# Key and value projections of a cross-attention stage as joint pairs: the last k-group by seven products, one core of a Trainium2 chip

## The chip, the cores and the metric

The kernel runs on one core of one Trainium2 chip. The core has a matrix engine (PE; its weight loads are listed apart as PEld), a vector engine (DVE), a scalar engine (ACT), a general-purpose engine (POOL) and a sync engine (SP) that issues most DMAs. Each engine works through its own instructions in a fixed order and waits on semaphores for the others. The metric is the device time of one execution in microseconds; less is better. About 0.2% (5.4 us here) is what a measurement of this kernel can tell from no change.

## The reference, cut to what matters

Two transformer blocks run one after the other on 256 tokens of width 2048, all in float32. The change lies in the memory cross-attention of the second block:

```python
def memory_cross_attention(h, mem_n, w_cq, w_ckv, w_co):
    q = (h @ w_cq).reshape(B, T, CROSS_HEADS, CROSS_HD)          # 4 heads of 512
    kv = (mem_n @ w_ckv).reshape(B, M, 2, CROSS_HEADS, CROSS_HD)
    k, v = kv[:, :, 0], kv[:, :, 1]
    s = jnp.einsum('bthd,bmhd->bhtm', q, k).astype(jnp.float32) * (CROSS_HD ** -0.5)
    pr = jax.nn.softmax(s, axis=-1).astype(v.dtype)
    o = jnp.einsum('bhtm,bmhd->bthd', pr, v).reshape(B, T, D_MODEL)
    return o @ w_co
```

`mem_n` is 256 memory rows of width 2048, normalised; `w_ckv` is 2048 x 4096. Columns 512h to 512h+511 give the keys of head h, columns 2048+512h onward its values.

## The kernel before

**Tiles.** A weight matrix is read in units of 512 rows x 512 columns (1 MB, one DMA into a `raw` tile; four of those exist). A unit is four k-tiles of 128 rows. A chunk is 512 output columns: its four units are the k-groups g = 0 to 3. Float32 precision is kept by splitting every operand in a high and a low part of type fp32r: ACT casts the high part (L235, `wh`), DVE subtracts to get the low one (L236, `wl`), half a unit (128 x 1024) at a time, at most five halves ahead (`WBUF`). A product of one k-tile then takes three matmuls of 512 columns (L280 to L282) for each of the two token tiles t, so a unit costs 24 matmuls.

**Pairs and seven products.** Two chunks that read the same activations can be computed as a pair (`pair8`). For k-groups 0 to 2 each chunk's units run as usual into four accumulators `c11`, `c21` (left chunk, token tiles 0 and 1) and `c12`, `c22` (right chunk). For the last k-group the two units and the activations are seen as a 2 x 2 times 2 x 2 block product, which Strassen's and Winograd's scheme does with seven block products in place of eight. Seven times six matmuls stand in place of 48. The price is paid elsewhere: DVE forms sums of weight blocks (`form`, four operations of 128 x 1024), seven halves are split in place of four, the activations' block sums are made once (`sums_job`, `four_sums`), and the results are put together by one copy on ACT (L376) and eight adds on DVE: L378 (first rows of the left chunk, tile `a`), L381, L383, L384 (`b`), L387, L389 (second rows of the left chunk, tile `c`), L391, L392 (second rows of the right chunk, tile `u`). The last of the seven products goes into `c21`, and L389 is the add that waits for it. `w_cq`, `w_in` and the first chunk of both feed-forwards already run in this way; `w_ckv` does not.

**The cross stage.** `cross` computes the four query chunks as two pairs. Then `gemm` (before) walks through eight chunks of `w_ckv` in the order key 0, value 0, key 1, value 1 and so on. When a key chunk is done, `on_k` scales it by the memory rows' normalisation on ACT (L505, `scaled`) and starts a `group_job`, which some k-tiles later (`wait`) flips it on PE (eight transposes, L490) and splits it (L472 on ACT, L473 on DVE). When the value chunk is done, `on_v` scales and splits the values (L1174, L1175) and starts `cross_job`: 24 matmuls of 256 columns for the scores S, softmax, four transposes (L1204), 24 matmuls for the output. `residual` then multiplies by `w_co`.

**What sets the order.** PE's order is the order in which the Python code emits instructions (`manual_schedule`); the other engines' order is set by the tile scheduler at build time and is fixed as well. Work beside the main stream is written as generators (jobs): `tick` after each k-tile lets each job count down its `yield n` and emit its next step. `spawn` runs a job's first step at once. `need(job)` runs a job to its end on the spot, whatever its wait. `cross_job` begins with `qT, kT = self.need(qT), self.need(kT)`.

Of the kernel before, what the change touches and what calls it, by code (L numbers as in the profile page):

```python
# [10 lines left out]
F32 = mybir.dt.float32  # L11
F32R = mybir.dt.float32r
# [71 lines left out]
class _Net:  # L84
# [87 lines left out]
    def plan(self):  # L172

        p, U = [], self.units
        self.seven = set()

        def add(chunks, late=False):
            p.extend(chunks[c][g] for c, g in self.order(chunks, late))

        def pair(a, b, seven):  # L180
            for g in range(len(a)):
                if g in seven:
                    self.seven.add(len(p))
                p.extend((b[g], a[g]))

        def ffn(gate, up, off, down, seven):
            for c, n, ks in self.ffn_steps():
                if n is not None:
                    add([U(down, n, ks)])
                else:  # L190
                    pair(U(gate, c), U(up, c + off), seven if c else (3,))
            add([U(down, n, PARTS[-1]) for n in range(4)])

        add([U("w_qkv", n) for n in (4, 0, 1, 2, 3)])
        add([U("w_o", n) for n in range(4)], True)
        ffn("w_gate", "w_up1", 0, "w_dn1", SEVEN1)
        for n in (0, 2, 6, 4):
            pair(U("w_in", n), U("w_in", n + 1), (3,))
        for ns in BRANCH:
            for n in ns:  # L200
                pair(U("w_in", 8 + n), U("w_in", 12 + n), (3,))
            add([U("w_br", n, (2 * j, 2 * j + 1)) for n in ns for j in range(2)])
        add([U("w_out", n) for n in range(4)], True)
        for n in (0, 2):
            pair(U("w_cq", n), U("w_cq", n + 1), (3,))
        add([U("w_ckv", 4 * j + h) for h in range(4) for j in range(2)])
        add([U("w_co", n) for n in range(4)], True)
        ffn("w_up2", "w_up2", 11, "w_dn2", SEVEN2)
        return p
# [113 lines left out]
            yield 2  # L323
        return out

    def four_sums(self, p, q):
        nc = self.nc
        s = self.s4([128, 8, 128])
        nc.vector.tensor_add(s[:, 0:2], q[:, 0:2], q[:, 2:4])
        nc.vector.tensor_sub(s[:, 2:4], s[:, 0:2], p[:, 0:2])  # L330
        nc.vector.tensor_sub(s[:, 4:6], p[:, 0:2], q[:, 0:2])
        nc.vector.tensor_sub(s[:, 6:8], p[:, 2:4], s[:, 2:4])
        yield 1
        h, l = (self.s4([128, 8, 128], F32R) for _ in range(2))
        nc.scalar.copy(h, s)
        nc.vector.tensor_sub(l, s, h.bitcast(F32))
        return [(h[:, z], l[:, z]) for z in (slice(0, 4), slice(4, 8))]

    def sums_job(self, acts):

        while len(acts) < 4 or not isinstance(acts[3], tuple) and not acts[3].done:
            yield 2
        h, l = self.need(acts[3])
        f = self.s4([128, 4, 256])
        self.nc.vector.tensor_add(f, h.bitcast(F32), l.bitcast(F32))
        yield 2
        return [(yield from self.four_sums(f[:, :, 0:128], f[:, :, 128:256]))]

    def pair8(self, left, right, acts, sums):

# [49 lines left out]
    def pair(self, left, right, acts, diffs, seven):  # L400

        nc = self.nc
        add = nc.vector.tensor_add
        acts = [self.need(z) for z in acts]
        p2, p4, p5, p3 = (self.bank(tag="acc") for _ in range(4))
        used = set()  # L410

        def product(o, z, k, t, stop):
            h, l = self.task()
            for i in range(2):
                self.mm(o, z, k + i, t, (h[:, i], l[:, i]), id(o) not in used, stop and i == 1)
                used.add(id(o))
            self.tick()

        o1 = None
        for g in range(len(acts)):  # L420
            A, S = acts[g], diffs[g]
            if g not in seven:
                for units in (right, left):
                    outs = ((p2, A, 0), (p4, A, 1)) if units is left else ((p5, A, 1), (p3, S, 0))
                    for k, w in enumerate(self.weights(units[g])):
                        for o, z, t in outs:
                            self.mm(o, z, k, t, w, id(o) not in used, False)
                            used.add(id(o))
                        self.tick()
                continue  # L430
            assert self.stream[self.used:self.used + 2] == [right[g], left[g]]
            self.used += 2
            if o1 is None:
                o1, o6, o7 = self.bank(), self.bank(), self.bank(tag="po")
            end = g == seven[-1]
            product(p3, S[1], 2, 0, end)
            product(o1, A, 0, 0, end)
            if end:
                u, a, b, c = (self.s2([128, 512]) for _ in range(4))
                nc.scalar.copy(u, o1)  # L440
            product(p2, A, 2, 0, end)
            if end:
                add(a, p2, u)
                yield a
            product(o6, S[0], 2, 0, end)
            if end:
                add(u, o6, u)
            product(p5, S[0], 0, 0, end)
            if end:
                add(b, p5, u)  # L450
                add(b, p3, b)  # L451
                yield b
            product(o7, S[1], 0, 0, end)
            if end:
                add(u, o7, u)
            product(p4, A, 2, 1, end)
        add(c, p4, u)
        add(u, p5, u)
        yield c
        yield u  # L460
# [509 lines left out]
    def gla_job(self, xacts, r, qk, pre):  # L970
# [88 lines left out]
        nc.vector.tensor_mul(k1, kT[:, 0], e)  # L1059
        yield 1  # L1060
        cross(*prev)
        e = self.s2([128, 4, 128])
        nc.scalar.activation(e, bT[:, 1], AF.Exp, scale=IG)
# [70 lines left out]
    def cross(self):  # L1134
        nc, a = self.nc, self.a
        r, xacts = self.r, self.xacts
        rq = self.sm([128, 2])
        nc.vector.tensor_scalar(rq, r, 512.0 ** -0.5, None, op0=ALU.mult)
        ss = self.sm([128, 2, 4])
        macts, qT, oacts, kT = [], [], [], []  # L1140

        def memory():

            yield 16
            for g in range(4):
                raws = [self.s2([128, 2, 256]) for _ in range(2)]
                self.load_flipped(raws, a["memT"][g])
                macts.append(self.spawn(self.input_job(raws, "g_mem_2", g, 4)))
                yield 6
            for t in range(2):  # L1150
                raws = [self.s2([128, 512]) for _ in range(4)]
                for i, raw in enumerate(raws):
                    nc.sync.dma_start(raw, a["mem"][0, t * 128:t * 128 + 128, i * 512:i * 512 + 512])
                yield 4
                for i, raw in enumerate(raws):
                    nc.scalar.activation(raw, raw, AF.Square, accum_out=ss[:, t, i:i + 1])
                yield 1
            return self.rstd(ss, D)

        rm = self.spawn(memory())  # L1160
        sums = self.spawn(self.sums_job(xacts))
        for n in (0, 2):
            for p in self.pairs8(self.units("w_cq", n), self.units("w_cq", n + 1), xacts, sums):
                qT.append(self.spawn(self.group_job(self.scaled(p, rq, p), wait=8)))
        rm = self.need(rm)

        def on_k(p):
            kT.append(self.spawn(self.group_job(self.scaled(p, rm))))

        def on_v(p):  # L1170
            hl = self.s4([128, 2, 512], F32R), self.s4([128, 2, 512], F32R)
            for t in range(2):
                h = hl[0][:, t]
                nc.scalar.activation(h, p[t], AF.Identity, bias=0.0, scale=rm[:, t:t + 1])  # L1174
                nc.vector.scalar_tensor_tensor(hl[1][:, t], p[t], rm[:, t:t + 1], h.bitcast(F32),  # L1175
                                               op0=ALU.mult, op1=ALU.subtract)
            h = len(oacts)
            oacts.append(self.spawn(self.cross_job(qT[h], kT[h], hl)))

        self.gemm([(self.units("w_ckv", 4 * j + h), f)  # L1180
                   for h in range(4) for j, f in enumerate((on_k, on_v))], macts)
        self.residual("w_co", range(4), oacts, "g_ffn_2", late=True)

    def cross_job(self, qT, kT, v):
# [203 lines left out]
```

## Time and profile before

| | us |
|---|---|
| median of 3 runs (2674.83 to 2677.06) | 2676.76 |
| the profiled execution | 2676.41 |
| its span, first to last instruction | 2674.6 |
| PE busy in the span | 2645.4 (99%) |
| DVE busy | 2044.5 (76%) |
| ACT busy | 1467.8 (55%) |

The profiled execution is 0.35 us under the median and 1.8 us longer than its span. In rows of matmuls the time given is modelled: they overlap, so the distance between two starts is what one costs. The same holds for DVE and ACT, where an instruction's successor may start some 0.1 us ahead of its end.

### The profile page before, as it was taken

To read this page: it belongs to the slowest core of one execution; us is meant where nothing else is said; L and a number is where in the kernel's file an instruction comes from. 1 tells how busy PE (TensorE), PEld (TensorE's weight loads), DVE (VectorE), ACT (ScalarE), POOL (GpSimd) and SP (SyncE) were. 2 spreads that over 40 slices of the span, in tenths; PEclk is the share of its full clock that TensorE was granted. 3 is DMA by queue.
4 is the path that set the end of the run, shared out by engine and by line. 5 is a ranking of instruction groups with operands and counts; after the bars stand their busy time and mean duration, and the time that the engine had idled before them with its cause. 6 is when DMAs were issued, how large, how long until landed. Compare 5 with 4: busy or idle time off the path is not lost.

```text
span 2674.6 us, 31765 instructions
## 1 busy us (share of the span) xinstructions
PE 2645.4 (99%) x12280; PEld 2180.7 (82%) x12280; DVE 2044.5 (76%) x2417; ACT 1467.8 (55%) x1899; POOL 27.7 (1%) x27
## 2 busy tenths in 40 slices
PE   8999999999999999999999999999999999999998
PEld 6778888888888887888888888888888888888887
DVE  7776899888888866977767577554588877777776
ACT  6565565555555555555445456444465655555554
POOL 0100000000000000000000000000000000000000
PEclk9999999999999999999999999999999999999999
DMA  7334454555555554355555556444554555555553
GB/s 297 122 118 150 173 206 184 207 204 192 205 208 199 195 194 162 126 205 193 200 189 191 187 200 241 168 162 160 186 189 173 197 195 191 190 191 194 195 193 140
DMA packets 74087, 499.61 MB, mean 187 GB/s; under 512 B 8496, under 2 KB 9392, under 8 KB 14928
## 3 DMA queue, kind: packets, MB, share of 16 engines
q1 hardware_dynamic: 73936, 497.59, 51.4%
q8 instruction: 96, 1.57, 0.2%
q14 instruction: 55, 0.45, 0.0%
HBM read 495.46 MB, written 2.10 MB: 186 GB/s over the span
## 4 chain that ended last, share of the span: by engine, by line
PE 92%; DVE 4%; issue 2%; ACT 1%; POOL 0%; DMA 0%; SPq 0%; DVEq 0%; POOLq 0%; ACTq 0%
PE acc L280 27%; PE acc L282 27%; PE acc L281 27%; PE aux L490 2%; PE aux L281 2%; PE aux L282 2%; PE aux L280 2%; DVE wl L236 1%; PE po L803 1%; PE po L280 1%; PE po L281 1%; PE po L282 1%; POOL sm L514 0%; PE aux L1036 0%; ACT wh L235 0%
## 5 line engine op out<-in xcount | busy, mean ns | idle before, releaser
L236 DVE TENSOR_TENSOR wl<-raw,wh 128x1024 fp32r<-128x1024 f32 (+1 forms) x1048 | 1272.3, 1220 | 527.9 <-ACT wh L235 515.7
L235 ACT CAST wh<-raw 128x1024 fp32r<-128x1024 f32 (+1 forms) x1048 | 1095.2, 1050 | 1033.7 <-PE acc L282 935.9
L280 PE MATMUL acc<-wh,s 128*128 128x512 f32 x3320 | 1317.8, 397 | 9.6 <-ACT wh L235 5.7
L282 PE MATMUL acc<-wh,s 128*128 128x512 f32 x3320 | 1295.5, 390 | 0.6 <-DVE s L473 0.6
L281 PE MATMUL acc<-wl,s 128*128 128x512 f32 x3320 | 1294.5, 390 | 0.3 <-DVE wl L236 0.3
L280 PEld LDWEIGHTS acc<-wh,s 128*128 128x128 f32 x3320 | 624.4, 188 | 147.9 <-DVE s L451 7.1
L282 PEld LDWEIGHTS acc<-wh,s 128*128 128x128 f32 x3320 | 623.8, 188 | 133.4 <-DVE s L473 1.1
L281 PEld LDWEIGHTS acc<-wl,s 128*128 128x128 f32 x3320 | 624.7, 188 | 123.1 <-DVE wl L236 1.7
L281 PE MATMUL aux<-wl,s 128*128 128x512 f32 x192 | 74.8, 390 | 0.7 <-DVE wl L236 0.7
L280 PE MATMUL aux<-wh,s 128*128 128x512 f32 x192 | 74.9, 390 | 0.0
L282 PE MATMUL aux<-wh,s 128*128 128x512 f32 x192 | 74.7, 389 | 0.0
L536 DVE TENSOR_TENSOR x<-acc,x 128x512 f32<-128x512 f32 x112 | 72.9, 683 | 0.0
L490 PEld LDWEIGHTS aux<-con,s 128*128 128x128 f32 x408 | 50.0, 140 | 14.3 <-issue 1.9
L490 PE MATMUL aux<-con,s 128*128 128x128 f32 x408 | 60.7, 272 | 0.7 <-DVE s L473 0.7
L472 ACT CAST s<-aux 128x512 fp32r<-128x512 f32 x66 | 38.3, 585 | 33.0 <-PE aux L490 23.0
L1233 ACT ACTIVATE s<-aux,vec 128x256 f32<-128x256 f32 x88 | 48.3, 562 | 13.6 <-PE aux L490 7.8
L514 POOL TENSOR_TENSOR sm<-sm,mhalf 128x2 f32<-128x2 f32 (+3 forms) x22 | 26.6, 1207 | 2641.2 <-DVE sm L522 2284.8
L256 DVE TENSOR_TENSOR raw<-raw 128x1024 f32<-128x1024 f32 x42 | 51.4, 1225 | 1.3
L473 DVE TENSOR_TENSOR s<-aux,s 128x512 fp32r<-128x512 f32 x66 | 44.5, 687 | 10.4 <-ACT s L472 10.2
L253 DVE TENSOR_TENSOR raw<-raw,raw 128x1024 f32<-128x1024 f32 x42 | 51.4, 1224 | 1.3
L252 DVE TENSOR_TENSOR raw<-raw 128x1024 f32<-128x1024 f32 x42 | 51.4, 1223 | 1.2
L254 DVE TENSOR_TENSOR raw<-raw,raw 128x1024 f32<-128x1024 f32 x42 | 51.4, 1223 | 1.2
(204 smaller groups left out, 1485.7 us busy)
## 6 DMA issues: line engine op xcount, KB each, us to landing
raw<-in_w_up SPq DMA_DIRECT2D x132, 1024.0 KB, 4.8
raw<-in_w_dn SPq DMA_DIRECT2D x88, 1024.0 KB, 4.9
raw<-in_w_in SPq DMA_DIRECT2D x64, 1024.0 KB, 4.8
raw<-in_w_gate SPq DMA_DIRECT2D x44, 1024.0 KB, 4.8
raw<-in_w_ckv SPq DMA_DIRECT2D x32, 1024.0 KB, 4.7
raw<-in_w_qkv SPq DMA_DIRECT2D x19, 1024.0 KB, 5.2
raw<-in_w_o SPq DMA_DIRECT2D x16, 1024.0 KB, 4.8
raw<-in_w_br SPq DMA_DIRECT2D x16, 1024.0 KB, 4.8
```

What stands on the lines that cost most here:

```text
L235: nc.scalar.copy(h[:, m], raw[:, m])
L236: nc.vector.tensor_sub(l[:, m], raw[:, m], h[:, m].bitcast(F32))
L252: nc.vector.tensor_sub(b22, b22, b12)
L253: nc.vector.tensor_sub(b12, b12, b11)
L254: nc.vector.tensor_add(b11, b11, b22)
L256: nc.vector.tensor_sub(b21, b21, b11)
L280: nc.tensor.matmul(o, ah[:, k, s], h, start=first, stop=False)
L281: nc.tensor.matmul(o, ah[:, k, s], l, start=False, stop=False)
L282: nc.tensor.matmul(o, al[:, k, s], h, start=False, stop=last)
L490: self.nc.tensor.transpose(b[:, j, t * 128:t * 128 + 128], srcs[t][:, (k + j) * 128:(k + j) * 128 + 128], self.ident)
L536: nc.vector.tensor_add(xs[t], pss[t], xs[t])
L1233: nc.scalar.activation(y[:, j], b[:, j], AF.Identity, bias=bb, scale=w2)
```

## The change

The four key chunks and the four value chunks become four pairs (key h with value h) in the plan and in `cross`. `four_sums` and `sums_job` get a form that keeps the memory's block sums in smaller tiles. `on_k` scales the keys in place, and its `group_job` is given a wait of twelve k-tiles (three before).

```diff
-        add([U("w_ckv", 4 * j + h) for h in range(4) for j in range(2)])
+        for h in range(4):
+            pair(U("w_ckv", h), U("w_ckv", 4 + h), (3,))
...
-    def four_sums(self, p, q):
+    def four_sums(self, p, q, small=False):
...
+        if small:
+            out = []
+            for z in (s[:, 0:4], s[:, 4:8]):
+                h, l = (self.s2([128, 4, 128], F32R) for _ in range(2))
+                nc.scalar.copy(h, z)
+                nc.vector.tensor_sub(l, z, h.bitcast(F32))
+                out.append((h, l))
+            return out
...
         def on_k(p):
-            kT.append(self.spawn(self.group_job(self.scaled(p, rm))))
+            kT.append(self.spawn(self.group_job(self.scaled(p, rm, p), wait=12)))
...
-        self.gemm([(self.units("w_ckv", 4 * j + h), f)
-                   for h in range(4) for j, f in enumerate((on_k, on_v))], macts)
+        sums = self.spawn(self.sums_job(macts, True))
+        for h in range(4):
+            k, v = self.pairs8(self.units("w_ckv", h), self.units("w_ckv", 4 + h), macts, sums)
+            on_k(k)
+            on_v(v)
+        del k, v, sums
```

Added lines shift the numbers: L280 becomes L281, L389 becomes L398, L472 L481, L473 L482, L490 L499, L505 L514, L1174 L1183, L1175 L1184. Over the whole program PE's order has 24 rows fewer, DVE's 67 more, ACT's 18 more.

The order changes most where a head's keys and values are finished; head 0 stands here, and the other three read alike. On PE before, the key chunk's last product (`acc2539`) is followed by twelve value matmuls (two k-tiles; the last four are shown, into `acc2570` and `acc2571`) ahead of the first four flips, which read the scaled keys `s2_2568` and `s2_2569`:

```order
L282 MATMUL acc2570_13051<-wh2561_12997,s4_2420_12325 128x512
L280 MATMUL acc2571_13052<-wh2561_12997,s4_2419_12324 128x512
L281 MATMUL acc2571_13052<-wl2562_12998,s4_2419_12324 128x512
L282 MATMUL acc2571_13052<-wh2561_12997,s4_2420_12325 128x512
L490 MATMUL aux2577_13073<-con_71,s2_2568_13047 128x128
L490 MATMUL aux2577_13073<-con_71,s2_2569_13048 128x128
L490 MATMUL aux2577_13073<-con_71,s2_2568_13047 128x128
L490 MATMUL aux2577_13073<-con_71,s2_2569_13048 128x128
L280 MATMUL acc2570_13051<-wh2563_13013,s4_2419_12324 128x512
```

The scores come 78 value matmuls after the last of the eight flips. On PE after, at the end of the first key and value pair (`acc2540` is `c21`, `s2_2590` and `s2_2592` the scaled keys `a` and `c`, `s4_2612` and `s4_2613` the flipped keys' high and low parts, `aux2616` the scores):

```order
L283 MATMUL acc2540_12880<-wh2599_13174,s4_2491_12656 128x512
L499 MATMUL aux2614_13237<-con_71,s2_2590_13138 128x128
L499 MATMUL aux2614_13237<-con_71,s2_2592_13140 128x128
L499 MATMUL aux2614_13237<-con_71,s2_2590_13138 128x128
L499 MATMUL aux2614_13237<-con_71,s2_2592_13140 128x128
L499 MATMUL aux2615_13244<-con_71,s2_2590_13138 128x128
L499 MATMUL aux2615_13244<-con_71,s2_2592_13140 128x128
L499 MATMUL aux2615_13244<-con_71,s2_2590_13138 128x128
L499 MATMUL aux2615_13244<-con_71,s2_2592_13140 128x128
L281 MATMUL aux2616_13251<-s4_2612_13235,s4_2470_12557 128x256
L282 MATMUL aux2616_13251<-s4_2613_13236,s4_2470_12557 128x256
```

The flips and the scores now stand directly behind the last of the seven products.

On DVE before, at the end of value chunk 0 (`acc2570`, `acc2571`), the values' low parts stand between splits, and the keys' splits lie far ahead of them:

```order
L236 TENSOR_TENSOR wl2605_13248<-raw2574_13057,wh2604_13247 128x1024
L1175 SCALAR_TENSOR_TENSOR s4_2597_13206<-acc2570_13051,sm2537_12875,s4_2596_13205 128x512
L1175 SCALAR_TENSOR_TENSOR s4_2597_13206<-acc2571_13052,sm2537_12875,s4_2596_13205 128x512
L236 TENSOR_TENSOR wl2611_13275<-raw2583_13107,wh2610_13274 128x1024
L1192 TENSOR_REDUCE sm2599_13236<-aux2598_13211 128x2
```

On DVE after, at the end of the first pair (`s2_2592` is `c`, `s2_2591` and `s2_2589` the value rows `b` and `u`, `po2588` a product bank, `acc2541` is `c22`):

```order
L396 TENSOR_TENSOR s2_2589_13137<-aux2587_13135,s2_2589_13137 128x512
L237 TENSOR_TENSOR wl2609_13215<-raw2578_13068,wh2608_13214 128x1024
L398 TENSOR_TENSOR s2_2592_13140<-acc2540_12880,s2_2589_13137 128x512
L1184 SCALAR_TENSOR_TENSOR s4_2611_13230<-s2_2591_13139,sm2537_12875,s4_2610_13229 128x512
L400 TENSOR_TENSOR s2_2589_13137<-po2588_13136,s2_2589_13137 128x512
L237 TENSOR_TENSOR wl2625_13290<-raw2578_13068,wh2624_13289 128x1024
L401 TENSOR_TENSOR s2_2589_13137<-acc2541_12881,s2_2589_13137 128x512
L482 TENSOR_TENSOR s4_2613_13236<-aux2614_13237,s4_2612_13235 128x512
L482 TENSOR_TENSOR s4_2613_13236<-aux2615_13244,s4_2612_13235 128x512
```

The keys' low parts (L482) now stand four instructions behind the add of `c`.

On ACT after, at the same place (`wh2627` is the fifth half of the next pair, `s4_2610` the values' high part):

```order
L236 CAST wh2627_13307<-raw2601_13178 128x1024
L1183 ACTIVATE s4_2610_13229<-s2_2591_13139,sm2537_12875 128x512
L514 ACTIVATE s2_2592_13140<-s2_2592_13140,sm2537_12875 128x512
L481 CAST s4_2612_13235<-aux2614_13237 128x512
L481 CAST s4_2612_13235<-aux2615_13244 128x512
```

The scaling of `c` (L514) and the keys' high parts (L481) follow each other with nothing between.

## Rows read from the trace of the kernel before

**Rows 1.** The page: engine totals (busy us, share, count) and PE clock per slice.
```profile
PE 2645.4 (99%) x12280; PEld 2180.7 (82%) x12280; DVE 2044.5 (76%) x2417; ACT 1467.8 (55%) x1899; POOL 27.7 (1%) x27
PEclk9999999999999999999999999999999999999999
```

**Rows 2.** Waits of PE: who for whom, us in total, times, longest.
```profile
PE acc L280 <- ACT wh L235: 5.7, 1, 5.7
...
PE aux L750 <- DVE s L699: 2.7, 2, 1.6
```

**Rows 3.** Busy time by stretch: key and value chunks, then granted clock, DMA.
```profile
1643.00:1847.00 204.00, 203.65 (x1005) 171.35 (x1004) 108.78 (x115) 96.73 (x121) 0.00 (x0) 1.00 0.51 177
```

**Rows 4.** Timeline of PE, end of second query pair: start, us, engine, line.
```profile
1641.65 0.39 PE L280 MATMUL acc<-wh,s 128*128 128x512 f32 x1
...
1642.78 0.39 PE L282 MATMUL acc<-wh,s 128*128 128x512 f32 x1
1643.01 0.39 PE L280 MATMUL acc<-wh,s 128*128 128x512 f32 x1
```

**Rows 5.** Timeline of DVE at the same place.
```profile
1644.24 1.22 DVE L236 TENSOR_TENSOR wl<-raw,wh 128x1024 fp32r<-128x1024 f32 x1
1645.37 0.68 DVE L389 TENSOR_TENSOR s<-acc,s 128x512 f32<-128x512 f32 x1
1645.97 1.22 DVE L236 TENSOR_TENSOR wl<-raw,wh 128x1024 fp32r<-128x1024 f32 x1
```

**Rows 6.** Timeline of ACT at the same place.
```profile
1643.20 1.05 ACT L235 CAST wh<-raw 128x1024 fp32r<-128x1024 f32 x1 [0.25 <-PE acc L282]
1644.16 0.72 ACT L505 ACTIVATE s<-s,sm 128x512 f32<-128x512 f32 x1
```

**Rows 7.** Timelines of PE, ACT and DVE: flips of queries and their splits.
```profile
1609.35 1.03 PE L490 MATMUL aux<-con,s 128*128 128x128 f32 x8
1610.13 0.48 PE L280 MATMUL acc<-wh,s 128*128 128x512 f32 x1
...
1656.38 0.60 PE L490 MATMUL aux<-con,s 128*128 128x128 f32 x4
...
1657.02 0.59 ACT L472 CAST s<-aux 128x512 fp32r<-128x512 f32 x1 [0.63 <-PE aux L490]
1658.02 0.59 ACT L472 CAST s<-aux 128x512 fp32r<-128x512 f32 x1 [0.42 <-PE aux L490]
...
1658.65 0.69 DVE L473 TENSOR_TENSOR s<-aux,s 128x512 fp32r<-128x512 f32 x1 [0.18 <-ACT s L472]
```

**Rows 8.** Timelines of DVE and PE, head 0: values' low parts, two scores.
```profile
1690.38 1.41 DVE L1175 SCALAR_TENSOR_TENSOR s<-acc,sm,s 128x512 fp32r<-128x512 f32 x2 [0.52 <-ACT s L1174]
...
1692.70 0.28 PE L281 MATMUL aux<-s,s 128*128 128x256 f32 x1
1692.82 0.28 PE L282 MATMUL aux<-s,s 128*128 128x256 f32 x1
```

**Rows 9.** Line L389 (duration min/median/max), and timelines of its latest case.
```profile
L389 DVE TENSOR_TENSOR s<-acc,s x12: 680/684/697, 323.8 to 1984.2; 128x512 f32<-128x512 f32 x12
...
1139.30 0.39 PE L282 MATMUL acc<-wh,s 128*128 128x512 f32 x1
...
1143.39 0.70 DVE L389 TENSOR_TENSOR s<-acc,s 128x512 f32<-128x512 f32 x1
```

**Rows 10.** Timeline of PE at the program's start.
```profile
5.70 0.80 PE L280 MATMUL acc<-wh,s 128*128 128x512 f32 x1 [5.70 <-ACT wh L235]
...
10.44 0.63 PE L281 MATMUL acc<-wl,s 128*128 128x512 f32 x1
10.86 0.54 PE L282 MATMUL acc<-wh,s 128*128 128x512 f32 x1
11.24 0.40 PE L280 MATMUL acc<-wh,s 128*128 128x512 f32 x1
```

**Rows 11.** Line L392, who waited for it: us in total, times.
```profile
  PEld acc L280: 1.5, 3
```

More of the change, by code (lines that the diff above doesn't have):

```diff
@@ L337, in four_sums, with sums_job @@
         return [(h[:, z], l[:, z]) for z in (slice(0, 4), slice(4, 8))]
-    def sums_job(self, acts):
+    def sums_job(self, acts, small=False):
         while len(acts) < 4 or not isinstance(acts[3], tuple) and not acts[3].done:
@@ L346, in sums_job @@
         yield 2
-        return [(yield from self.four_sums(f[:, :, 0:128], f[:, :, 128:256]))]
+        return [(yield from self.four_sums(f[:, :, 0:128], f[:, :, 128:256], small))]
     def pair8(self, left, right, acts, sums):
```

## Prediction

> **What bounds the kernel now.** I read the page first. PE is busy 99% of the span, DVE 76%, ACT 55% [rows 1], so time is PE's: matmuls taken out shorten the program only as far as PE does not wait instead. The view of waits comes next. PE waits once for 5.7 us at the start; no later single wait is over 1.6 us [rows 2]. Then the stage itself: in the 204.0 us from the first key matmul to the start of `w_co`, PE is busy 203.65, DVE 108.78, ACT 96.73 [rows 3]. PE has no gap there that a change could fill, and both other engines have room on average. So two questions decide: what the removed matmuls are worth, and whether PE still finds its operands ready at each step of its fixed order. For the second I read the timelines at the end of the second query pair, which already runs as a pair with seven products: it shows how far DVE and ACT are behind PE at such a place [rows 4 to 6].
>
> **What is removed.** Each pair's last k-group takes 42 matmuls in place of 48, four pairs save 24. From the start of the six matmuls of a last product to the start of the next one pass 1643.01 - 1641.65 = 1.36 us [rows 4], 0.227 us each. 24 x 0.227 = **5.4 us saved**, all on PE and so on the path. That is 0.20% of 2676.
>
> **What is added beside PE.** Per pair, DVE gets three more splits and four forming operations of 128 x 1024 at 1645.37 - 1644.24 = 1.13 us each, and eight adds of 128 x 512 at 1645.97 - 1645.37 = 0.60 us each [rows 5]: 7 x 1.13 + 8 x 0.60 = 12.7 us, 51 us for four pairs. The block sums of the memory (seven more DVE operations, two on ACT) come once, a few us. DVE would stand near 165 of some 200 us, ACT, with four more instructions per pair of at most 1.05 us [rows 6], near 114. On average both stay hidden under PE; PE ran through the query pairs' ends under the same load. Nothing is added to a DMA queue: the same 32 units, fetched key and value alternately. The first key pair now follows a query pair as a pair, using all four accumulators; weight loads waited 1.5 us in three cases for the add that frees the last one [rows 11], so 0 to 0.5 us, taken as 0.2.
>
> **What is moved: the wait of twelve k-tiles does not hold.** `on_v(v)` follows `on_k(k)` at once, `on_v` spawns `cross_job`, a spawned job runs its first step on the spot, and that step is `need(kT)`, which runs the flips to their end whatever wait they were given. The order of the changed program shows it: the eight flips, and behind them the 24 score matmuls, stand directly behind the last product into `c21`. Before, twelve value matmuls stood between a key chunk and its flips, and 78 more between the last flip and the scores; these covered ACT's and DVE's work on the keys. Now that cover is gone, and PE waits through the whole chain: add of `c` on DVE, scaling on ACT, flips on PE, cast on ACT, subtraction on DVE. Queued behind on PE are the scores and then the whole next pair (or `w_co`); nothing else can pass.
>
> I work the chain out on the clock of the query pair, where PE's next matmul started at 1643.01 [rows 4].
>
> 1. DVE reaches the add of `c` (L389) at 1645.37 and ends it at 1646.05 [rows 5], though the product's last matmul began at 1642.78 and ended at 1643.17 [rows 4]. DVE is 2.2 us behind, because splits for the next pair and the other adds stand ahead of it. The instructions ahead of it are the same in the changed order.
> 2. ACT: the cast of the fifth half can start when the last product frees its buffer, 1643.20, and a scaling follows at 1644.16 [rows 6]. In the changed order the first values' scaling takes that place, so ACT is free by 1644.9, and the scaling of `c` runs from 1646.1 for 0.72 us, to 1646.8.
> 3. PE: flips start near 1646.85. Four flips that started at 1656.38 had their cast start at 1657.02, 0.64 us later [rows 7]. So the first cast runs at 1647.5 and ends, after 0.59 us, at 1648.1. The second four flips and their cast follow at once.
> 4. DVE: behind the add of `c` stand the values' low part (near 0.7 us: two took 1.41 [rows 8]), an add (0.60), a split (1.13) and the add of `c22` (0.60). From 1645.97 that gives 1649.0. DVE is still behind: the keys' subtraction could start at 1648.1 (a subtraction followed its cast by 0.04 us [rows 7]) and starts at 1649.0. It takes 0.69 us, to 1649.7.
> 5. The second score matmul needs that low part. Without a wait it would start at 1643.01 plus 0.78 us for eight flips (1609.35 to 1610.13 [rows 7]) plus 0.12 us for one score matmul [rows 8], 1643.9. It starts at 1649.7. The second subtraction ends 0.6 us later, when PE, six score matmuls on, first needs it.
>
> The **new wait is 5.8 us per head**. All four heads read alike in the order, also the last, where `w_co` follows. 4 x 5.8 = **23.2 us added**. Bounds: had DVE no work between the add and the subtraction, the low part would be there at 1648.8, a wait of 4.9; had it in addition been free to add at 1643.2, the wait would be 2.7. Upward, of twelve such adds the latest started 1143.39 - 1139.69 = 3.7 us after the last matmul's end (1139.30 + 0.39) [rows 9] instead of 2.2, which gives 7.3. I take 5.8, since the place it is read from is the same pattern one pair earlier, with the same queue. Nothing gives this back later: PE had no waits in the stage that a head start of DVE and ACT could remove. Behind the scores, the softmax has three k-tiles until its flips where it had two; it becomes no tighter.
>
> **Sum.** On the profiled execution: 2676.4 - 5.4 + 23.2 + 0.2 = 2694.4; the median of the runs is 0.35 higher, so **2694.7 us**, 0.7% slower.
>
> **A clock that falls.** At the program's start, after 5.70 us without a matmul, starts lie 0.42 us apart (10.44 to 10.86) and reach the usual 0.23 from 11.24 on [rows 10]: 512 columns at 1.2 and then at 2.4 GHz. The page shows the granted clock at full from then on [rows 1], but it has no PE gap of more than 1.6 us to test it [rows 2]. The changed program has, per head, 3.7 us with nothing on PE (1643.17 to 1646.85), a short burst of flips, and about 2 us with one matmul. If PE fell back to 1.2 GHz each time, it would pay what the start paid: twelve matmuls took 11.24 - 5.70 = 5.54 us instead of 12 x 0.227 = 2.72, so up to 2.8 us per head, 11 us in all: 2706. The Trainium skill, page "TensorE: Matmul & The Clock Gate", section "HAM oscillation — how this bites in real kernels", says that a matmul kernel which idles between bursts falls back to half clock in the gap and pays the warm-up anew at every burst. By that rule the change would pay at all four heads; no run here shows it yet.
>
> **Rivals.**
>
> - *The clock falls in the waits* (all heads 2706, one or two 2697 to 2700). For it: the start. Against it: the longest empty stretch is shorter than the start's, and flips lie in between. 0.25.
> - *The wait is shorter because DVE is not behind*: the scheduler's order is the same, but after an earlier wait DVE may have run ahead. With bounds of 2.7 to 4.9 us per head: 2682 to 2691. Against it: DVE's backlog at such a place is made in the last k-group itself, in each pair anew. 0.09.
> - *The flips do run later, under the next pair's k-tiles, as the wait says.* Then PE never waits and the saving stands: 2676.8 - 5.4 + 0.2 = 2671.6, faster. It decides from 5.4 / 4 = 1.36 us of wait per head: below that the change gains. Against it stand the code path and the order of the changed program; even with empty queues the chain alone (0.68 + 0.72 + 0.64 + 0.59 + 0.69 us, less 0.9 us of PE's own flips and first score) is over that. 0.03.
> - *DVE becomes the bound in the last k-groups* with block sums and scores' work on top, so that weights come late as well (2701, by the upward bound of 7.3). For it: one case of 3.7 us among twelve. 0.05.
>
> **How the numbers follow.** The forecast, 2694.7 with some 3 us around it, has 0.58. The range of eight in ten reaches up to the clock's case and down to a wait of 4.6 us: 2690 to 2707. Faster by over 0.2% (below 2671.4) or within 0.2% (to 2682.1) needs the third rival, whose 2671.6 lies on the edge between the two, or the low end of the second: 0.02 and 0.03. Slower: 0.95.
>
> **What would show it.** Right: PE's order as given, and in the waits four cases of PE on L499 (flips) of about 3.7 us each, for ACT's L514 or DVE's L398, and four on L282 in the scores of 1.5 to 2 us for DVE's L482; 24 matmuls fewer; PE's busy share down by some 15 us of gaps; starts 0.227 us apart behind the scores. The clock rival shows as starts of 0.42 us behind a wait. Wrong: flips standing between the next pair's k-tiles, waits of under 1.4 us per head, or a cast of the fifth half that waits long for its DMA and moves the scaling of `c` with it.

## The result and the profile after

The changed kernel takes **2702.62 us** (median), the kernel before 2676.41 in the same comparison: ratio 1.0099, 95% interval 1.0087 to 1.0111. It is 26.2 us slower, where 18.0 were forecast. The time lies inside the range (2690 to 2707), but 7.9 us above the forecast (2694.7) and near the numbers of two rivals, 2701 (DVE as the bound) and 2706 (a falling clock); the profile tells them apart.

The page after, engine totals (busy us, share, count), and the row of PE's clock per slice:

```profile
span 2700.4 us, 31831 instructions
...
PE 2654.4 (98%) x12256; PEld 2187.6 (81%) x12256; DVE 2098.3 (78%) x2484; ACT 1483.8 (55%) x1917; POOL 27.7 (1%) x27
...
PEclk9999999999999999999999999899999999999999
```

Against [rows 1] PE has 24 instructions fewer and is yet busy 9.0 us *longer*. That is the first sign: waits alone would leave the busy time shorter. The clock row, all nines before, has an eight in one slice.

Who PE waited for (engine, tile and line, releaser: us in total, times, longest). The first and the last line are new groups; between them stands the longest single wait of the program, the one at its start:

```profile
PE aux L499 <- ACT s L514: 14.3, 4, 3.6
PE acc L281 <- ACT wh L236: 5.1, 1, 5.1
...
PE aux L282 <- DVE s L482: 3.1, 4, 1.0
```

In [rows 2] there was no single wait over 1.6 us behind the start. Now PE waits four times for the scaling of `c` (the flips) and four times for the keys' low part (the second score).

Where the time lies: I measure the stage from the start of the last query-pair matmul into `po` to the first flip behind `w_co`. PE's timelines, before (first two lines) and after (last two):

```profile
1640.06 0.39 PE L282 MATMUL po<-wh,s 128*128 128x512 f32 x1
...
1889.68 0.38 PE L490 MATMUL aux<-con,x 128*128 128x128 f32 x2
```
```profile
1639.27 0.39 PE L283 MATMUL po<-wh,s 128*128 128x512 f32 x1
...
1915.31 0.27 PE L499 MATMUL aux<-con,x 128*128 128x128 f32 x1
```

The stage took 249.62 us and takes 276.04: +26.42, all of the loss.

The end of the first pair, on PE (start, us, engine, line, then idle time before and its releaser):

```profile
1687.12 0.39 PE L283 MATMUL acc<-wh,s 128*128 128x512 f32 x1
1687.36 0.27 PE L499 MATMUL aux<-con,s 128*128 128x128 f32 x1
1691.21 1.76 PE L499 MATMUL aux<-con,s 128*128 128x128 f32 x7 [3.58 <-ACT s L514]
1692.79 0.58 PE L281 MATMUL aux<-s,s 128*128 128x256 f32 x1
1694.05 0.58 PE L282 MATMUL aux<-s,s 128*128 128x256 f32 x1 [0.68 <-DVE s L482]
...
1698.69 0.41 PE L282 MATMUL aux<-s,s 128*128 128x256 f32 x1
1698.91 0.41 PE L283 MATMUL aux<-s,s 128*128 128x256 f32 x1
1699.12 0.63 PE L281 MATMUL acc<-wh,s 128*128 128x512 f32 x1
1699.55 0.63 PE L282 MATMUL acc<-wl,s 128*128 128x512 f32 x1
...
1700.26 0.39 PE L281 MATMUL acc<-wh,s 128*128 128x512 f32 x1
1700.49 0.40 PE L282 MATMUL acc<-wl,s 128*128 128x512 f32 x1
```

The flip of `a` starts at once, at 1687.36; the next one, which needs `c`, starts 3.85 us later. From there on everything is slow: flips 0.23 us apart instead of 0.10, scores of 256 columns 0.21 instead of 0.12 [rows 8], the next pair's first matmuls 0.43 instead of 0.23. Only at 1700.26 is the usual pitch back. DVE and ACT at the same place:

```profile
1689.72 0.68 DVE L398 TENSOR_TENSOR s<-acc,s 128x512 f32<-128x512 f32 x1
...
1693.31 1.27 DVE L482 TENSOR_TENSOR s<-aux,s 128x512 fp32r<-128x512 f32 x2
```
```profile
1690.43 0.72 ACT L514 ACTIVATE s<-s,sm 128x512 f32<-128x512 f32 x1 [1.21 <-DVE s L398]
1692.15 0.59 ACT L481 CAST s<-aux 128x512 fp32r<-128x512 f32 x1 [0.99 <-PE aux L499]
```

Busy time by stretch (stretch and length; PE, PEld, DVE, ACT, POOL busy with counts; granted clock; DMA share; GB/s): before the wait, the wait and the flips, the scores, and behind the next pair's start; then the ends of the other three heads:

```profile
1642.00:1687.00 45.00, 44.59 (x203) 36.31 (x202) 35.62 (x38) 25.81 (x31) 0.00 (x0) 1.00 0.53 186
1687.00:1693.00 6.00, 2.42 (x12) 1.80 (x10) 6.00 (x9) 3.28 (x5) 0.00 (x0) 0.74 0.71 268
1693.00:1697.00 4.00, 3.32 (x15) 3.03 (x16) 3.38 (x5) 2.49 (x3) 0.00 (x0) 0.50 0.73 262
...
1701.00:1745.00 44.00, 44.00 (x209) 36.87 (x208) 28.31 (x29) 21.27 (x25) 0.00 (x0) 1.00 0.39 132
...
1749.00:1757.00 8.00, 7.27 (x32) 6.76 (x33) 5.22 (x7) 1.79 (x3) 0.00 (x0) 0.50 0.43 152
1807.00:1815.00 8.00, 7.32 (x36) 6.63 (x37) 5.80 (x8) 1.96 (x4) 0.00 (x0) 0.64 0.39 147
1863.00:1871.00 8.00, 6.60 (x31) 5.97 (x32) 5.54 (x8) 2.21 (x4) 0.00 (x0) 0.57 0.46 170
```

A granted clock of 0.50 is 1.2 GHz, 1.00 is 2.4. It is full up to the wait and falls at all four heads. At the first two it is half through all the scores and back when the next pair is under way; at the third and fourth it is back before the scores end (their last ones lie 0.12 us apart again). And PE's row shows why "busy" misleads here: in the scores' stretch it is busy 3.32 of 4.00 us, at half speed.

### The profile page after: what moved, and what is told of

Same layout as the page of the kernel before. It is cut to its first block, busy times and chain, and to the rows that moved or that the text cites. A ratio compares the mean times of both kernels' runs of the same rounds, so it can differ in the third digit from the quotient of the medians.

```text
span 2700.4 us, 31831 instructions
## 1 busy us (share of the span) xinstructions
PE 2654.4 (98%) x12256; PEld 2187.6 (81%) x12256; DVE 2098.3 (78%) x2484; ACT 1483.8 (55%) x1917; POOL 27.7 (1%) x27
## 4 chain that ended last, share of the span: by engine, by line
PE 91%; DVE 5%; issue 2%; ACT 1%; POOL 0%; DMA 0%; SPq 0%; DVEq 0%; POOLq 0%; ACTq 0%
PE acc L281 27%; PE acc L283 26%; PE acc L282 26%; PE aux L282 2%; PE aux L499 2%; PE aux L283 2%; PE aux L281 2%; DVE wl L237 1%; PE po L812 1%; PE po L283 1%; PE po L282 1%; PE po L281 1%; POOL sm L523 0%; PE aux L1045 0%; ACT wh L236 0%
## 5 line engine op out<-in xcount | busy, mean ns | idle before, releaser
L236 ACT CAST wh<-raw 128x1024 fp32r<-128x1024 f32 (+1 forms) x1060 | 1107.6, 1050 | 1028.0 <-PE acc L283 936.7
L237 DVE TENSOR_TENSOR wl<-raw,wh 128x1024 fp32r<-128x1024 f32 (+1 forms) x1060 | 1285.8, 1218 | 491.2 <-ACT wh L236 478.6
L281 PE MATMUL acc<-wh,s 128*128 128x512 f32 x3280 | 1302.1, 397 | 8.9 <-ACT wh L236 5.1
L283 PE MATMUL acc<-wh,s 128*128 128x512 f32 x3280 | 1280.2, 390 | 0.6 <-DVE s L482 0.6
L282 PE MATMUL acc<-wl,s 128*128 128x512 f32 x3280 | 1279.4, 390 | 0.3 <-DVE wl L237 0.3
L281 PEld LDWEIGHTS acc<-wh,s 128*128 128x128 f32 x3280 | 617.3, 188 | 146.4 <-DVE s L460 7.1
L283 PEld LDWEIGHTS acc<-wh,s 128*128 128x128 f32 x3280 | 616.6, 188 | 132.1 <-DVE s L482 1.1
L282 PE MATMUL aux<-wl,s 128*128 128x512 f32 x216 | 84.2, 390 | 0.7 <-DVE wl L237 0.7
L281 PE MATMUL aux<-wh,s 128*128 128x512 f32 x216 | 84.2, 390 | 0.0
L283 PE MATMUL aux<-wh,s 128*128 128x512 f32 x216 | 84.1, 389 | 0.0
L499 PE MATMUL aux<-con,s 128*128 128x128 f32 x408 | 63.5, 281 | 15.0 <-ACT s L514 14.3
L499 PEld LDWEIGHTS aux<-con,s 128*128 128x128 f32 x408 | 51.5, 145 | 29.2 <-ACT s L514 15.8
L481 ACT CAST s<-aux 128x512 fp32r<-128x512 f32 x66 | 38.3, 585 | 35.7 <-PE aux L499 24.5
L257 DVE TENSOR_TENSOR raw<-raw 128x1024 f32<-128x1024 f32 x46 | 56.3, 1225 | 1.4
L254 DVE TENSOR_TENSOR raw<-raw,raw 128x1024 f32<-128x1024 f32 x46 | 56.3, 1225 | 1.4
L253 DVE TENSOR_TENSOR raw<-raw 128x1024 f32<-128x1024 f32 x46 | 56.3, 1224 | 1.4
L255 DVE TENSOR_TENSOR raw<-raw,raw 128x1024 f32<-128x1024 f32 x46 | 56.3, 1223 | 1.3
L486 ACT ACTIVATE s<-aux,vec 128x256 fp32r<-128x256 f32 x80 | 37.8, 474 | 22.3 <-PE aux L499 13.1
```

The costliest lines, as they stand in the source:

```text
L236: nc.scalar.copy(h[:, m], raw[:, m])
L237: nc.vector.tensor_sub(l[:, m], raw[:, m], h[:, m].bitcast(F32))
L253: nc.vector.tensor_sub(b22, b22, b12)
L254: nc.vector.tensor_sub(b12, b12, b11)
L255: nc.vector.tensor_add(b11, b11, b22)
L257: nc.vector.tensor_sub(b21, b21, b11)
```

## The experiments

My theory after these readings: each head pays the chain that the prediction worked out (5.8 us), and about 2 us of half clock on top; both go if the flips come late enough. The rival: the loss is the pairing itself (more work on DVE, all four accumulators in use), and the clock's fall is an accompaniment without a price.

The stage is read in each kernel's own profile, between the same two rows, medians and ratios from comparisons with the kernel before (2676.4 to 2676.6).

| kernel | median us | ratio, 95% interval | stage us | against before |
|---|---|---|---|---|
| before | 2676.41 | | 249.62 | |
| after | 2702.62 | 1.0099 [1.0087, 1.0111] | 276.04 | +26.42 |
| scores 16 k-tiles later | 2672.93 | 0.9986 [0.9977, 0.9995] | 245.28 | -4.34 |
| flips 6, scores 10 later | 2672.56 | 0.9985 [0.9977, 0.9994] | 245.32 | -4.30 |
| waits filled | 2694.38 | 1.0069 [1.0054, 1.0085] | 267.66 | +18.04 |
| only the last head forced | 2679.33 | 1.0013 [1.0004, 1.0022] | 253.00 | +3.38 |
| only the flips forced | 2692.32 | 1.0059 [1.0043, 1.0076] | 267.16 | +17.54 |
| flips 2, scores 3 later | 2684.68 | 1.0031 [1.0019, 1.0043] | 258.52 | +8.90 |

**Scores later.** The job for the scores gives its first step away, so that the wait of twelve k-tiles holds.

```diff
     def cross_job(self, qT, kT, v):
...
+        yield 16
         qT, kT = self.need(qT), self.need(kT)
```

> The changed kernel, with a wait of 16 k-tiles ahead of the first step of cross_job, so that nothing forces the flips and they stand twelve k-tiles into the next pair (or into w_co), the scores sixteen. Theory (the loss is the forced flips: per head a wait of PE of 5.8 us at full clock and about 2 us of half clock behind it): all of it goes, the 24 matmuls stay saved, 2676.4 - 5.4 + 0.2 = 2671.2 us, granted clock 0.999, no wait of PE on flips over 0.5 us. Rival (the loss is the added work of DVE and ACT or the four accumulators that a pair takes): the wait moves to weights or accumulators, 2680 us or more.

It is faster than before, and 29.7 us faster than the change. So the pairing itself costs no such sum, and the forcing is the whole loss. The gain is smaller than the 0.2% that a measurement can tell from no change, but both versions with later flips show it, in the medians and in the stage, and their intervals lie below 1. The stage saves 4.34 us where 5.4 less 0.2 was expected; what is missing is found below.

**The same with smaller numbers**: six k-tiles until the flips, ten until the scores.

```diff
-            kT.append(self.spawn(self.group_job(self.scaled(p, rm, p), wait=12)))
+            kT.append(self.spawn(self.group_job(self.scaled(p, rm, p), wait=6)))
...
+        yield 10
         qT, kT = self.need(qT), self.need(kT)
```

> As the run before it, but the flips six k-tiles later and cross_job ten. Theory: DVE and ACT need some 4 us from the end of the last product to the scaled keys, three k-tiles of 1.36 us, so six are enough: 2671.2 us, within 1 us of the run with twelve and sixteen. Rival (DVE is so far behind at a pair's start that twelve are needed): waits of PE on flips or scores of 1 us or more per head, 2675 us or more.

The same within 0.4 us. PE runs from the last product (its last matmul starts at 1686.30) straight into the next pair, at 1686.52; three matmuls later the pair takes up its second accumulator, at 1687.30:

```profile
1686.30 0.39 PE L283 MATMUL acc<-wh,s 128*128 128x512 f32 x1
1686.52 0.39 PE L281 MATMUL acc<-wh,s 128*128 128x512 f32 x1
...
1686.97 0.39 PE L283 MATMUL acc<-wh,s 128*128 128x512 f32 x1
1687.30 0.50 PE L281 MATMUL acc<-wh,s 128*128 128x512 f32 x1
1687.64 0.39 PE L282 MATMUL acc<-wl,s 128*128 128x512 f32 x1
```

No wait of 3.6 us is left; the flips' largest group in the view of waits is this, and the stretch of the key and value pairs stands under it:

```profile
PE aux L499 <- DVE s L482: 0.7, 2, 0.3
```
```profile
1640.00:1847.00 207.00, 206.59 (x1001) 172.17 (x1000) 162.84 (x179) 115.23 (x140) 0.00 (x0) 1.00 0.49 179
```

The clock is full, DVE has 162.84 us of 207.00 and ACT 115.23. The step from 1686.97 to 1687.30 is 0.33 us and the next one 0.34, each 0.1 more than the usual 0.227: two starts that come late at the pair's edge. The view of weight loads' waits shows for what; first this kernel, then the kernel before (L384 and L393 are the same add, into `b`, which frees `c12`; L392 and L401 the add of `c22`):

```profile
PEld acc L281 <- DVE s L393: 7.4, 16, 1.9
...
PEld acc L281 <- DVE s L401: 1.9, 4, 0.5
```
```profile
PEld acc L280 <- DVE s L384: 6.0, 12, 1.9
```

Four more cases, 1.4 us more, and for `c22` four in place of three [rows 11]. On PE's timeline of the stage 27 matmuls start 0.3 us or more after the one before them, 2.99 us in all beyond the pitch of 0.227, against 17 with 1.82 before. The 1.17 us between them are the missing part of the saving: each of the four edges behind a key and value pair costs about 0.2 us, and the first pair behind the query pair 0.34.

**Waits filled.** The clock is tested by giving PE work it doesn't need: 33 matmuls of 256 columns into the scores' bank (which the true scores then overwrite) ahead of the forced flips.

```diff
-        qT, kT = self.need(qT), self.need(kT)
+        qT = self.need(qT)
...
+        for z in range(11):
+            self.mm(S[:, 0], qT, z % 4, z % 2, [y[:, z % 2] for y in qT], True, True)
+        kT = self.need(kT)
```

> The changed kernel, with 33 matmuls of 256 columns that nobody needs (queries times queries, into the scores' bank, overwritten by the scores) between the last product and the forced flips of each head. They take 33 x 0.12 = 4.0 us, about the 3.6 us for which PE otherwise stands still there. Theory (half clock behind the wait is a cost of its own): PE stays at 2.4 GHz, the waits that are left are of 1 to 2 us, and the time is the forecast's, 2676.4 - 5.4 + 0.2 + 23.2 + 4 x 0.3 = 2695.6 us, 7 us less than the changed kernel though more is computed. Rival (the clock costs nothing, since PE would wait for the keys anyway): 2703 us or more.

More work, and 8.2 us faster than the change. PE around the flips, and the clock there:

```profile
1688.58 0.39 PE L283 MATMUL acc<-wh,s 128*128 128x512 f32 x1
...
1692.76 1.03 PE L499 MATMUL aux<-con,s 128*128 128x128 f32 x8
...
1695.50 0.39 PE L282 MATMUL aux<-s,s 128*128 128x256 f32 x1 [1.09 <-DVE s L482]
```
```profile
1691.00:1697.00 6.00, 4.67 (x37) 4.24 (x37) 6.00 (x10) 3.80 (x5) 0.00 (x0) 1.00 0.62 224
```

The clock stays at 1.00, the flips run 0.10 us apart. PE's slot behind the last product is 1688.80 (1688.58 + 0.22); without a wait the second score would start 0.90 us later, at 1689.70; it starts at 1695.50, **5.80 us late**. This is the forecast's wait with the clock taken out, and the median (2694.38) is the forecast's (2694.7). The difference to the change, 8.2 us in the medians and 8.38 in the stage, is what the clock cost: 2.1 us per head on the mean.

**Only the last head forced.** The other three (`h < 3`) take the 16 k-tiles.

```diff
-            oacts.append(self.spawn(self.cross_job(qT[h], kT[h], hl)))
+            oacts.append(self.spawn(self.cross_job(qT[h], kT[h], hl, h < 3)))
...
-    def cross_job(self, qT, kT, v):
+    def cross_job(self, qT, kT, v, later):
...
+        if later:
+            yield 16
```

> As the first run, but the last head's flips and scores are forced as in the changed kernel, ahead of w_co. Theory: one head's share comes back, (2702.6 - 2671.2) / 4 = 7.8 us: 2679.0 us, with one wait of PE of 3.6 us for the scaled keys and one stretch at 1.2 GHz. Rival (the loss sits where a pair follows a pair, so that the last head, with w_co behind it, has none): 2671 to 2673 us.

```profile
PE aux L499 <- ACT s L514: 3.6, 1, 3.6
```
```profile
1841.00:1848.00 7.00, 5.72 (x28) 5.19 (x27) 4.67 (x6) 1.80 (x3) 0.00 (x0) 0.54 0.44 154
```

One wait, one fall of the clock (0.54 in that window). Against all heads late the stage is 7.72 us longer and the median 6.4. In the change, with four heads forced, the stage is 30.76 us longer, a quarter of which is 7.69: the heads pay one by one, and what one loses, none gives back.

**Only the flips forced.** The flips stand behind the last product as in the change, the scores come 16 k-tiles later.

```diff
             kT.append(self.spawn(self.group_job(self.scaled(p, rm, p), wait=12)))
+            self.need(kT[-1])
...
+        yield 16
         qT, kT = self.need(qT), self.need(kT)
```

> The changed kernel with the flips forced directly behind the last product, as it has them, but the scores sixteen k-tiles into the next pair. It leaves PE the first of the two waits per head (for the add and the scaling of c) and takes away the second (for the keys' low part). Theory: 3.84 us of wait per head, 4 x 3.84 = 15.4 us over the run with flips and scores later (2672.6): 2688.0 us if the clock stays, and up to 2 us more per head, 2696 us, if PE falls to 1.2 GHz in a wait of this length alone. Rival (the scores' wait, not the flips', carries the loss): 2680 us or less.

```profile
PE aux L499 <- ACT s L514: 14.4, 4, 3.6
```
```profile
1686.00:1692.00 6.00, 2.73 (x13) 1.98 (x11) 6.00 (x8) 3.59 (x4) 0.00 (x0) 0.97 0.95 373
1692.00:1698.00 6.00, 5.68 (x17) 4.81 (x18) 5.49 (x8) 2.67 (x5) 0.00 (x0) 0.50 0.61 218
```

The one wait is enough to bring the clock down; the whole matmuls behind it run at half speed although PE has work from then on (17 in 6 us). These rows are of the first head, whose half clock lasted longest (6.8 us); at the other three it lasted half as long. Against the flips at six k-tiles the stage is 21.84 us longer, 5.5 per head: 3.86 from slot to second flip, 0.1 of it the first flip itself, and the rest, some 1.7 on the mean, the clock. (The profiled execution is the longest of its four; in the medians it is 19.8 us, 4.9 per head.) The change's second wait, for the scores' low part, with the half clock that goes on behind it, makes the other 2.2 us per head (26.42 against 17.54).

**Two k-tiles.** Half of the cover.

```diff
-            kT.append(self.spawn(self.group_job(self.scaled(p, rm, p), wait=12)))
+            kT.append(self.spawn(self.group_job(self.scaled(p, rm, p), wait=2)))
...
+        yield 3
         qT, kT = self.need(qT), self.need(kT)
```

> Flips two k-tiles (2.7 us) after the last product, scores three. Theory: the scaled keys are ready 3.84 us after PE's next free slot, so the flips wait 3.84 - 2.72 = 1.1 us, and the scores some 0.9 us for the second half's low part: 2 us per head, and no wait long enough for the clock to fall: 2672.6 + 8 = 2680.6 us. Rival (any distance of a k-tile or two is enough, as in the kernel before, whose flips stand two k-tiles behind): 2673 us.

The direction held, not the size: 3.3 us per head against six k-tiles ((258.52 - 245.32) / 4), where 2 were expected. Waits, then ACT's timeline at head 0, then the clock at and behind the waits:

```profile
PE aux L499 <- ACT s L514: 6.8, 4, 1.7
...
PE aux L282 <- DVE s L482: 3.7, 4, 0.9
```
```profile
1690.32 1.04 ACT L236 CAST wh<-raw 128x1024 fp32r<-128x1024 f32 x1 [1.34 <-PE acc L283]
1691.27 0.72 ACT L514 ACTIVATE s<-s,sm 128x512 f32<-128x512 f32 x1
```
```profile
1687.00:1692.00 5.00, 3.33 (x15) 2.19 (x13) 5.00 (x8) 3.40 (x5) 0.00 (x0) 1.00 0.81 301
1692.00:1698.00 6.00, 5.04 (x33) 4.38 (x34) 5.37 (x7) 3.16 (x4) 0.00 (x0) 1.00 0.49 175
```

The scores waited 0.9 us as expected, the flips 1.7 where 1.1 were: with two k-tiles in between, the cast of the next half stands on ACT ahead of the scaling of `c`, itself waiting for PE, and the scaling starts at 1691.27 instead of about 1690.2 (the add of `c` started at 1689.47, and in the change the scaling starts 0.71 us behind it). From start to start the two waits cost 1.87 and 1.19 us per head, which is nearly all of the 3.3. The clock stayed at 1.00: a PE wait of 1.7 us, flips, and one of 0.9 did not bring it down here; one of 3.6 did in three kernels, nine times of nine.

## Why the prediction was right or wrong

**The mechanism was right.** PE stands behind the last product as its order said, and the rival in which the flips come later (2671.6) is the time of a kernel in which they are made to (2672.56 and 2672.93).

That the time fell inside the range is owed to the clock's case, up to which the range was drawn; the forecast, "2694.7 with some 3 us around it", missed.

**The steps of the chain on which PE waits were right to 0.05 us.** From PE's slot behind the last product, 1687.36: the add of `c` starts 2.36 us later (forecast 1645.37 - 1643.01 = 2.36), the second flip 3.85 (3.84), the keys' subtraction 5.95 (5.99). Only the first cast came late, 4.79 us from the slot where step 3 has 4.5, since the flips ran at half clock; DVE was later still, so it cost nothing. At the other heads the flips' gap reads 3.85 or 3.86 too. It was right to read DVE's backlog at the query pair, where the same instructions stand ahead; DVE had not run ahead. Nor did it become the bound, though that rival's 2701 is the number next to the result: from 1640 to 1875 DVE is busy 163.13 of 235.00 us, and PE and its weight loads wait for no weights in the stage.

**Step 5 was right too.** The second score starts 5.80 us late with the waits filled, and 5.79 in the change itself (1694.05 against 1687.36 + 0.90): there the half clock stretches the flips into time that PE would have waited anyway. What the forecast left out lies behind that score: the other scores at 0.21 us in place of 0.12, and the first whole matmuls at 0.43 in place of 0.23, until 1700.26.

**The step that failed is the weighing of the clock**, which stands in the sum with nothing and to which I gave 0.25. I held against it that the longest empty stretch is shorter than the one at the start, and that flips lie in between. Neither counted: the first three falls came by the time the flips did, and the fall came at all four heads. [rows 10] could show only that PE *starts* at half clock, and no row of the kernel before showed a gap between 1.6 and 5.7 us. The Trainium skill's rule (page "TensorE: Matmul & The Clock Gate", section "HAM oscillation — how this bites in real kernels"), that a matmul kernel which idles between bursts falls to half clock in the gap and pays the warm-up anew, spoke for a fall at all four heads. The trace agrees with it: 0.50 after each of four waits of 3.6 us. In the run with two k-tiles it stayed at 1.00 behind waits of 1.7 us. The price that I had for the rival, up to 2.8 us per head, was sized well: 2.1 measured.

**The terms of the sum**, in the stage:

| term | forecast | measured | from |
|---|---|---|---|
| 24 matmuls less | -5.4 | -5.5 | flips at six k-tiles against before, -4.3, less the next row |
| accumulators at the pairs' edges | +0.2 | about +1.2 | late starts, 2.99 against 1.82 us |
| waits, four heads | +23.2 | +22.3 | waits filled, against flips at six k-tiles |
| clock | 0 | +8.4 | the change against waits filled |
| sum | +18.0 | +26.4 | the change against before |

The accumulators were mis-sized: I counted one new edge, of a key pair behind a query pair; there are also those of each key and value pair behind another and of `w_co` behind the last. In the change the pause hides most of it (its weight loads wait for L393 once in the stage, those with flips at six k-tiles five times; so the waits measure 22.3 and not 23.2, against a kernel that pays it), and in a kernel without the pause it takes a fifth of the gain.

What the change was able to give is thus 0.15% (0.9985, interval 0.9977 to 0.9994), with flips at six k-tiles, scores at ten. That version beats both kernels.

## What to carry to other kernels

A wait given to a job holds only until someone asks for its result: when work is postponed, look at who needs it first, and read the order that comes out. A wait on a full TensorE can have two prices, its length and the half clock behind it (here waits of 3.6 us had both, waits of 1.7 us only the first), and the second belongs in the sum, or in the chances, where the gap is longer than any that the trace shows at full clock; where such a wait can't be avoided, matmuls that nobody needs can be cheaper than silence (33 of them per head gave back 8.2 us here).

## What the runs showed of the hardware

The clock's fall reached past the wait that caused it: after the first pair PE had half clock until 1700.08 (by the trace's record of the clock), 8.9 us after the flips had come, and all through it had flips, scores and then whole matmuls, with one more wait of 0.7 us. At the last two heads it came back sooner, while the scores were still running.

The clock also fell at a place that has nothing to do with the change, near the program's start, in the profiles of three kernels (scores later, waits filled, only the flips forced) and not in the others. The same window in the kernels with scores later and with six k-tiles:

```profile
17.00:20.40 3.40, 3.40 (x10) 2.63 (x9) 3.40 (x6) 3.27 (x6) 0.00 (x0) 0.50 1.00 401
```
```profile
17.00:20.40 3.40, 3.40 (x17) 2.82 (x16) 3.40 (x7) 3.09 (x7) 0.00 (x0) 1.00 1.03 410
```

Ten matmuls in place of 17, so 7 x 0.227 = 1.6 us. It explains most of why these two profiled executions differ by 2.5 us (2673.03 and 2670.55) while their stages are equal (245.28 and 245.32). In the three kernels that show it PE had waited 1.3 us for ACT shortly before, in the others 0.6 to 1.2; yet the kernel with two k-tiles waited 1.7 us later on at full clock. What decides it was not tested.
